# Four tiles of stationary operands placed at the other end of SBUF in a decoder layer

## The chip, the core and the metric

The program runs on one core of a Trainium2 chip. A core has TensorE for matmuls, VectorE, ScalarE and GpSimd for work on vectors, SyncE for issuing DMAs, a memory of 128 partitions by 224 KiB (SBUF) for operands and a small one (PSUM) into which matmuls accumulate. The metric is the device time of one execution in microseconds.

## What is computed

The reference is one decoder layer on 256 tokens of width 2048, in float32:

```python
x = x + 0.5 * swiglu(rms_norm(x, ffn1_norm), ffn1_w_gate, ffn1_w_up, ffn1_w_down)    # D_FF = 5632
h = rms_norm(x, mix_norm)
proj = h @ w_in                     # split among three groups of heads
...                                 # gated linear attention, sparse attention, attention to 256 memory tokens
x = x + concat([o_gla, o_nsa, o_mem]) @ w_out
x = x + 0.5 * swiglu(rms_norm(x, ffn2_norm), ffn2_w_gate, ffn2_w_up, ffn2_w_down)
return rms_norm(x, final_norm)
```

The matmul work is in the two feed-forward networks (three matrices of 2048 by 5632 each), the projections `w_in`, `w_mem_kv` and `w_out`.

## The kernel before

Each float32 operand of a large product is split into two fp32r parts, a rounded value and the rest (`h` and `l` for weights), and a product becomes three matmuls: `mm3` (L301 to L304) multiplies the high part of the stationary side by the high part of the moving side (L302), by the low part (L303), and the low part of the stationary side by the high part of the moving side (L304). I call such three matmuls a triple. The weights stream: a DMA brings a chunk of 128 by 1024 into a tile `r`, ScalarE rounds it into `h` (L288), VectorE takes the difference `l` (L289), and both are moving operands, 512 columns at a time. The stationary side is 128 by 128: activations.

Those activations stay in SBUF in tiles of 16 KB per partition, 16 blocks of 128 by 256, made by the helper `t16` from the pool `p_t16`, which has four buffers and is open for the whole program. The pairs follow one another: `hh`, `hl` (input of the first network), `sh`, `sl` (sums and differences of its quarters), `xh`, `xl` (input of the projections), `oh`, `ol` (output of the heads), `zh`, `zl` and again `sh`, `sl` (second network); `sa`, `sb` and `gfin` borrow a buffer too. Blocks of 128 columns of them are what the weight load reads. Of the ten projections of `xh`, `xl` eight have 512 columns, one 296 and one 256.

The network runs in 11 slabs of 512 hidden columns. A slab after the first multiplies with seven products in place of eight for three quarters of its depth, and between its groups it puts in the down products of the slab before. For those the hidden values lie in the tile `gx`, 8 KB from a stage pool, high half and low half side by side, and `gx` is the stationary side. The seven products and the plain ones use `hh`, `hl`, `sh`, `sl` (`zh`, `zl` in the second network). A product of six matmuls is `product7`, the down products are `fill`.

The pools are opened in this order: `const`, `keep` (with `acc`, the residual), `p_t16`, `sm` (small values), and then, one stage after another, the pools of the first network, of the mixing part and of the second network. The stage pools are closed and opened again by `stage`, which means that a tile of a new stage waits for the last users of the earlier tile on the same bytes. All pools without a side grow from the low end of SBUF. In the compiled program the first 16 KB are taken by descriptors; `ident` of `const` begins at 0x4080, `acc` at 0x7ca0, the four buffers of `p_t16` at 0xbe00, 0xfe00, 0x13e00 and 0x17e00, `sm` at 0x1be00 and the stage pools at 0x1c340: in the networks `r` from there, `h` from 0x27340, `l` from 0x2d340, `gx` at 0x33340 and `wk` (tiles such as `c` and `g`) from 0x35340 to 0x37b40. In the mixing part `mT` and `qT` lie at multiples of 64 bytes and the two `kT` at 0x368a0 and 0x370e0, that is 32 past a multiple of 64; the last tile ends at 0x37d20. The range that the allocator may use ends at 0x37fe0, 32 bytes below 224 KiB.

The pools' line and the helper that takes tiles from the pool are:

```python
    const, keep, p_t16 = mk("const"), mk("keep"), mk("t16", 4)
...
    def t16(name, dt=F32R):
        return p_t16.tile([128, 16, 256], dt, name=name, tag="t16")
```

Of the kernel before, what the change touches and what calls it, by code (L numbers as in the profile page):

```python
# [186 lines left out]
def _body(tc, A):  # L187
# [1 line left out]
    act, dve, pool, pe = nc.scalar, nc.vector, nc.gpsimd, nc.tensor  # L189
    ctx = ExitStack()  # L190
    mk = lambda n, b=1, **k: ctx.enter_context(tc.tile_pool(name=n, bufs=b, **k))
    const, keep, p_t16 = mk("const"), mk("keep"), mk("t16", 4)
    sm = mk("sm", 3)
    P, sizes = {}, {}

# [1028 lines left out]
```

## Time and profile before

| | |
|---|---|
| median of 3 runs | 1881.18 us (1879.79 to 1882.1) |
| profiled execution | 1881.27 us |
| its span, first to last instruction | 1879.5 us |
| TensorE busy, matmul | 1840.5 us, 98% of the span |
| TensorE busy, weight load | 1486.1 us, 79% |
| VectorE busy | 1642.3 us, 87% |
| ScalarE busy | 1086.0 us, 58% |
| DMA | 397.34 MB, 211 GB/s |
| mean granted clock of TensorE | 0.994 of full |

The profile is one execution. Busy time of TensorE is the sum of matmuls whose ends are modelled and which overlap, so a matmul of 389 ns may follow another after 229; the distance from start to start is what counts, and I call it the spacing. The weight load has an engine row of its own (PEld), since it runs beside the matmul before.

### The profile page before, as it was taken

Reading aid. Unit: us, or ns where it says so; the run is one execution under the profiler, and the core shown is the slowest. Engines: PE = TensorE matmul, PEld = TensorE weight load, DVE = VectorE, ACT = ScalarE, POOL = GpSimd, SP = SyncE. Lnnn points to the kernel's source line nnn. Section 1 sums busy time; section 2 is a strip of 40 time slices with the busy share of each in tenths; the row PEclk is TensorE's granted clock in tenths of the full one; section 3 lists DMA queues with packets and bytes.
Section 4 is the critical chain, followed back from the end, with each engine's and each line's share of the span. In section 5 each row is a group of like instructions: output and inputs, shape, how many; then the busy total and the mean of one; then the engine's idle time right before and its main releaser. Section 6 shows DMA issues by size and latency. Waiting matters only on the chain.

```text
span 1879.5 us, 23784 instructions
## 1 busy us (share of the span) xinstructions
PE 1840.5 (98%) x8465; PEld 1486.1 (79%) x8465; DVE 1642.3 (87%) x2101; ACT 1086.0 (58%) x1376; POOL 84.6 (5%) x109
## 2 busy tenths in 40 slices
PE   8989999999999999999999999999999999999997
PEld 5868888888888877777777787888888888888885
DVE  7999999999999985576577854999999999999995
ACT  7446665656565656533456744566556655666563
POOL 0000000000000000001010000000000000000000
PEclk9999999999999999999999999999999999999999
DMA  9768777767776754545744453876777677767771
GB/s 333 228 190 261 253 225 235 247 202 226 236 249 197 229 169 158 188 150 177 247 157 130 163 181 117 295 239 209 213 237 255 203 214 238 253 201 216 239 246 49
DMA packets 111655, 397.34 MB, mean 211 GB/s; under 512 B 12592, under 2 KB 12848, under 8 KB 111408
## 3 DMA queue, kind: packets, MB, share of 16 engines
q1 hardware_dynamic: 102896, 364.36, 55.4%
q0 software_dynamic: 8640, 31.46, 9.7%
q8 instruction: 66, 1.08, 0.2%
q14 instruction: 53, 0.43, 0.1%
HBM read 393.68 MB, written 2.10 MB: 211 GB/s over the span
## 4 chain that ended last, share of the span: by engine, by line
PE 91%; DVE 5%; ACT 1%; issue 1%; POOL 1%; ACTq 0%; POOLq 0%; DVEq 0%
PE pm L303 20%; PE pm L302 20%; PE pm L304 20%; PE px L303 8%; PE px L302 8%; PE px L304 8%; DVE l L289 1%; PE pt L391 1%; PE pm L854 1%; PE px L819 0%; POOL y L326 0%; PE pt L339 0%; DVE exg L910 0%; PE po L1047 0%; POOL y L325 0%
## 5 line engine op out<-in xcount | busy, mean ns | idle before, releaser
L288 ACT ACTIVATE h<-r 128x1024 fp32r<-128x1024 f32 (+1 forms) x838 | 877.8, 1052 | 660.3 <-PE pm L304 491.6
L289 DVE TENSOR_TENSOR l<-r,h 128x1024 fp32r<-128x1024 f32 (+1 forms) x838 | 990.7, 1207 | 137.7 <-ACT h L288 129.3
L303 PE MATMUL px<-l,gx 128*128 128x512 f32 x624 | 243.2, 390 | 1.7 <-DVE l L289 1.7
L302 PE MATMUL px<-h,gx 128*128 128x512 f32 x624 | 243.2, 390 | 0.0
L304 PE MATMUL px<-h,gx 128*128 128x512 f32 x624 | 242.9, 389 | 0.0
L303 PE MATMUL pm<-l,sh 128*128 128x512 f32 x480 | 191.9, 400 | 2.3 <-DVE l L289 2.3
L302 PE MATMUL pm<-h,sh 128*128 128x512 f32 x480 | 190.1, 397 | 0.3 <-ACT h L288 0.3
L304 PE MATMUL pm<-h,sl 128*128 128x512 f32 x480 | 188.0, 392 | 0.0
L303 PE MATMUL pm<-l,hh 128*128 128x512 f32 x364 | 144.8, 398 | 3.6 <-DVE l L289 3.6
L302 PE MATMUL pm<-h,hh 128*128 128x512 f32 x364 | 142.4, 395 | 4.4 <-ACT h L288 4.4
L303 PE MATMUL pm<-l,zh 128*128 128x512 f32 x364 | 144.3, 396 | 0.1
L302 PE MATMUL pm<-h,zh 128*128 128x512 f32 x364 | 143.3, 394 | 0.0
L304 PE MATMUL pm<-h,zl 128*128 128x512 f32 x364 | 142.2, 391 | 0.0
L304 PE MATMUL pm<-h,hl 128*128 128x512 f32 x364 | 142.2, 391 | 0.0
L303 PEld LDWEIGHTS px<-l,gx 128*128 128x128 f32 x624 | 117.2, 188 | 26.7 <-DVE l L289 2.4
L302 PEld LDWEIGHTS px<-h,gx 128*128 128x128 f32 x624 | 117.2, 188 | 25.4 <-ACT h L288 0.2
L304 PEld LDWEIGHTS px<-h,gx 128*128 128x128 f32 x624 | 117.2, 188 | 24.2
L303 PE MATMUL pm<-l,xh 128*128 128x512 f32 (+2 forms) x320 | 120.7, 377 | 1.5 <-DVE l L289 1.5
L302 PE MATMUL pm<-h,xh 128*128 128x512 f32 (+2 forms) x320 | 121.3, 380 | 0.0
L304 PE MATMUL pm<-h,xl 128*128 128x512 f32 (+2 forms) x320 | 121.0, 379 | 0.0
L402 DVE SCALAR_TENSOR_TENSOR acc<-px,acc 128x512 f32<-128x512 f32 x156 | 106.9, 685 | 8.3 <-PE px L304 7.9
L302 PEld LDWEIGHTS pm<-h,sh 128*128 128x128 f32 x480 | 90.6, 189 | 20.5 <-ACT h L288 0.9
(329 smaller groups left out, 2641.0 us busy)
## 6 DMA issues: line engine op xcount, KB each, us to landing
r<-ffn1u SPq DMA_DIRECT2D x88, 512.0 KB, 4.9
r<-ffn1d SPq DMA_DIRECT2D x88, 512.0 KB, 4.9
r<-ffn2u SPq DMA_DIRECT2D x88, 512.0 KB, 4.7
r<-ffn2d SPq DMA_DIRECT2D x88, 512.0 KB, 4.8
r<-ffn1g SPq DMA_DIRECT2D x87, 512.0 KB, 5.0
r<-ffn2g SPq DMA_DIRECT2D x87, 512.0 KB, 5.1
r<-wout SPq DMA_DIRECT2D x32, 512.0 KB, 3.4
r<-ffn1u POOLq DMA_DIRECT2D x30, 512.0 KB, 7.3
```

The source lines that it names most:

```text
L288: act.activation(h[:, sl], r[:, sl], AF.Copy)
L289: dve.tensor_sub(l[:, sl], r[:, sl], f(h[:, sl]))
L302: pe.matmul(out, ah, wh, start=first, stop=False)
L303: pe.matmul(out, ah, wl, start=False, stop=False)
L304: pe.matmul(out, al, wh, start=False, stop=last)
L391: pe.transpose(pt[:, k], g[:, k * 128:k * 128 + 128], ident)
L402: dve.scalar_tensor_tensor(a, pd, 0.5, a, op0=ALU.mult, op1=ALU.add)
L854: pe.matmul(pcs[n][32 * p:32 * p + 32], flats[n][:, c * 4 + p], r[:, p * 256:p * 256 + 256], start=c == 0, stop=c == 7, tile_position=(0, ...
```

## The change

The pool of the four tiles is opened with a side. Its tiles then come from the high end of SBUF, above everything that the other pools take; the pools that are opened after it (`sm` and the stage pools) move down by the 64 KB that it leaves. `const` and `keep` stay in place. Nothing else is edited.

```diff
-    const, keep, p_t16 = mk("const"), mk("keep"), mk("t16", 4)
+    const, keep, p_t16 = mk("const"), mk("keep"), mk("t16", 4, side="right")
```

## Rows read from the trace of the kernel before

**Rows 1.** Table of stages: stretch, its us, busy us by engine, granted clock, DMA.
```profile
130.00:200.00 70.00, 65.16 (x278) 52.82 (x277) 68.01 (x83) 37.59 (x39) 2.59 (x3) 0.95 0.72 230
200.00:300.00 100.00, 100.00 (x448) 82.47 (x447) 98.49 (x100) 65.06 (x71) 4.31 (x5) 1.00 0.75 247
700.00:760.00 60.00, 56.59 (x287) 45.34 (x288) 36.00 (x59) 37.78 (x71) 3.64 (x6) 0.97 0.46 155
1100.00:1180.00 80.00, 78.34 (x347) 62.24 (x347) 43.33 (x54) 38.94 (x60) 0.89 (x2) 0.98 0.45 160
```

**Rows 2.** Chain that ended last, by engine, share of the span.
```profile
PE 91%; DVE 5%; ACT 1%; issue 1%; POOL 1%; ACTq 0%; POOLq 0%; DVEq 0%
```

**Rows 3.** Groups by line, one matmul of each triple: count | busy us, mean ns.
```profile
L303 PE MATMUL pm<-l,sh 128*128 128x512 f32 x480 | 191.9, 400 | 2.3 <-DVE l L289 2.3
L303 PE MATMUL pm<-l,hh 128*128 128x512 f32 x364 | 144.8, 398 | 3.6 <-DVE l L289 3.6
L303 PE MATMUL pm<-l,zh 128*128 128x512 f32 x364 | 144.3, 396 | 0.1
L303 PE MATMUL pm<-l,xh 128*128 128x512 f32 (+2 forms) x320 | 120.7, 377 | 1.5 <-DVE l L289 1.5
L303 PE MATMUL pm<-l,oh 128*128 128x512 f32 x128 | 51.2, 400 | 0.0
L303 PE MATMUL px<-l,hh 128*128 128x512 f32 x40 | 15.8, 394 | 0.0
L303 PE MATMUL px<-l,zh 128*128 128x512 f32 x40 | 15.8, 394 | 0.0
L303 PE MATMUL px<-l,gx 128*128 128x512 f32 x624 | 243.2, 390 | 1.7 <-DVE l L289 1.7
L303 PE MATMUL pm<-l,gx 128*128 128x512 f32 x80 | 32.0, 400 | 0.0
```

**Rows 4.** Timeline of TensorE, first and last matmul of three runs: start, duration.
```profile
250.27 0.39 PE L302 MATMUL pm<-h,hh 128*128 128x512 f32 x1
...
265.15 0.39 PE L304 MATMUL pm<-h,sl 128*128 128x512 f32 x1
...
304.60 0.39 PE L302 MATMUL px<-h,gx 128*128 128x512 f32 x1
...
307.10 0.39 PE L304 MATMUL px<-h,gx 128*128 128x512 f32 x1
...
1838.53 0.39 PE L302 MATMUL pm<-h,gx 128*128 128x512 f32 x1
...
1843.75 0.39 PE L304 MATMUL pm<-h,gx 128*128 128x512 f32 x1
```

**Rows 5.** Table of stages for the first and last of these runs.
```profile
250.26:265.16 14.90, 14.90 (x67) 12.22 (x66) 14.54 (x17) 8.52 (x9) 0.00 (x0) 1.00 0.45 135
1838.52:1843.75 5.23, 5.23 (x25) 4.32 (x24) 4.04 (x6) 1.95 (x2) 0.00 (x0) 1.00 0.00 0
```

**Rows 6.** Instructions of single lines: duration ns min/median/max, first and last start.
```profile
L303 PEld LDWEIGHTS px<-l,gx x624: 187/188/190, 71.5 to 1821.4; 128*128 128x128 f32 x156
L303 PEld LDWEIGHTS pm<-l,sh x480: 187/188/337, 63.6 to 1825.5; 128*128 128x128 f32 x160
L339 PEld LDWEIGHTS pt<-ident,acc x64: 137/140/143, 710.2 to 1172.5; 128*128 128x128 f32 x64
L391 PEld LDWEIGHTS pt<-ident,c x160: 137/141/231, 134.4 to 1847.8; 128*128 128x128 f32 x160
L999 PE MATMUL px<-kT,qT x16: 379/380/484, 978.5 to 1043.7; 128*128 128x256 f32 x16
L1126 PE MATMUL px<-mT x16: 378/380/459, 1062.8 to 1075.2; 128*128 128x256 f32 x16
```

## What I predict

> **What bounds the kernel now.** I read three views, in this order. First the table of stages: in a stretch of a feed-forward network TensorE is busy all the time at the full granted clock, while VectorE, the next one, is at 98.49 of 100 us and ScalarE at 65 [rows 1]. Then the chain that ended last: 91% of it is TensorE [rows 2], so the end is set by the number of matmuls times the spacing of their starts, and a wait only counts where TensorE stands still. Then the matmuls themselves: the groups of one line of the helper [rows 3] are one matmul of each triple, so the tiles that the change moves (hh, hl, sh, sl, xh, xl, zh, zl, oh, ol) are the stationary side of 480 + 364 + 364 + 320 + 128 + 40 + 40 = 1736 triples, that is 5208 matmuls; gx, which the change moves with the stage buffers, serves 624 + 80 = 704 triples, 2112 matmuls.
>
> **What the change removes, adds and moves.** It names no operation, no loop and no DMA, so the instruction counts stay. The four tiles are one pool that is open for the whole program; no other pool has ever used its bytes, before or after, so no buffer is handed over that was not handed over before. `sm` and the stage pools slide down together by 65,536 bytes and keep their places relative to each other, so each stage tile still lands on the same earlier tiles. I cost the waits of the buffers at nothing for that reason. Of the queues, SP keeps its DMAs and POOL its accumulating ones; a DMA to another address of the same 128 partitions has the same packets. What is left are the addresses, and an address can only matter in how long an operand takes to read or write.
>
> The largest reader is the matmul with its weight load, and here the trace has two values for the same shape. A run of 66 matmuls on hh, hl, sh and sl starts at 250.27 and its last one at 265.15 us: 14.88 us / 65 = 228.9 ns from start to start [rows 4, 5]. A run of 24 on gx goes from 1838.53 to 1843.75: 5.22 / 23 = 227.0 ns, and 12 on gx in the middle of a network from 304.60 to 307.10: 2.50 / 11 = 227.3 ns [rows 4, 5]. So gx is about 2 ns quicker per matmul, at the same moving buffers, clock and width. The weight load isn't what differs: 188 ns median for gx and for sh [rows 6], some 40 ns below the spacing, which hides it.
>
> What could make those 2 ns? The place is one candidate (gx lies at the top, 0x33340, the four tiles lie below the stages, from 0xbe00). Against it speaks that the four tiles span 64 KB themselves, and that the matmuls on hh and those on zh, which lie 32 KB apart, take 394 ns alike where they accumulate in px [rows 3]. The contents are another (gx holds the hidden values), and so is the layout (gx keeps both halves in one tile, the others in two). The change touches the first only. I take 0 ns as the value, and keep both ends: -2 ns if the new place has the spacing of gx, +2 ns if the move costs as much as the two places differ now.
>
> The second thing an address can alter is its offset. The four tiles start at a multiple of 512 bytes now. The allocator's usable range ends 32 bytes below 224 KiB, so from the other end they start at 0x27fe0 or a little lower; a block of 128 weights then starts 32 bytes past a multiple of 64. The trace has such operands today: acc lies at 0x7ca0, 32 past a multiple of 64, and the weight load of its transposes takes 140 ns median, that of the tile c, at a multiple of 64, 141 [rows 6]. With the moving side it is the same: kT lies 32 bytes off and mT doesn't, and the 256-wide matmuls take 380 ns and 380 [rows 6]. So I cost the offset at nothing too; if this cover were gone, the load has 40 ns of slack before the spacing grows. ScalarE's and VectorE's writes into the four tiles are few beside their work on h and l, and both engines have slack [rows 1].
>
> One rule of the Trainium skill bears on the 2 ns. The rows show equal loads and unequal spacings [rows 4, 6]. The page TensorE: Matmul & The Clock Gate (Part 2: What happens when you issue a matmul) says that TensorE has two independent read ports, so that loading the next weights takes nothing from the running matmul. By that rule the place of the stationary side is worth nothing and the time stays; by the row, read as an effect of the place, it would fall as in the first rival. The rule doesn't explain why gx is quicker.
>
> **The sum.** Profiled time 1881.27 us, span 1879.5, so 1.8 us lie around it. Changes: operations 0, waits 0, spacing 5208 x 0 + 2112 x 0, offset 0. That gives 1881.27; the median of the runs shown is 1881.18 (1879.79 to 1882.1), and I forecast **1881.2 us**. What can still move without a cause: the granted clock is 0.95 of full over 130 to 200 us, 0.97 over 700 to 760 and 0.98 over 1100 to 1180 [rows 1], that is 3.5, 1.8 and 1.6 us of lost full speed where TensorE had stood still for parts of the stretch; it falls to 1.2 from 2.4 GHz there. One such fall more or less is worth about 2 us, so the forecast alone reaches from 1878.5 to 1884.
>
> **The rivals.** *Faster: the quick spacing belongs to the place.* The four tiles then cover 0x27fe0 to 0x37fe0, where gx lies today, and gx goes down to 0x23340. From the groups, 8 of the 10 projections are 512 wide, so 5016 of the 5208 matmuls are; 5016 x -2 ns = -10.0 us, and gx loses 2112 x 2 ns = +4.2. Net -5.8: **1875.4 us**. If only the upper half of the four tiles gains, it is -5.0 + 4.2, and that lies within the forecast. For it: the rows show the 2 ns. Against it: the buffers of hh and zh lie 32 KB apart and take the same 394 ns [rows 3], and contents and layout explain it as well. VectorE wouldn't stop it, since it has 1.5 us of 100 left and TensorE would need less than 1% of it.
>
> *Slower: the 32-byte offset costs on every load.* Place: the weight loads of the four tiles in all three products. If the block of 512 bytes takes one piece more and TensorE's start waits for that, the price is at most what the trace shows between two sources, 2 ns: 5016 x 2 = +10.0 us, **1891.2 us**. It decides from 3.8 us / 5016 = 0.75 ns per matmul. For it: only that the fp32r loads of this shape are nowhere 32 bytes off in the trace. Against it: acc and kT, which are, and the 40 ns of slack.
>
> *The change isn't only one of addresses.* If the planner that orders the instructions sees other buffer edges, a wait could come or go. The forecast takes it that it does not, because no bytes change hands; this would show as another number of waits and either sign. I count its small chance with the two others.
>
> **How the numbers follow.** The forecast has 0.72, the faster rival with the favourable mishaps 0.15, the slower one with the others 0.13. About 0.2%, 3.8 us, is what a measurement of this kernel can tell from no change, and the forecast lies inside it while both rivals lie outside. So faster 0.15, same 0.72, slower 0.13. The range takes the forecast and the faster rival whole and the smaller half of the slower one's price: 1874 to 1886.5. Some 0.1 of the slower rival is left out above, and a few hundredths below.
>
> **What would show it.** Right: the same instruction counts, a slab run of 66 matmuls still at 228.9 ns, 24 on gx still at 227.0, weight loads at 188. The faster rival shows as runs on hh and sh below 228.2 and gx near 229; the slower one as runs above 229.7, perhaps with loads above 188. A different order shows as other waits of TensorE at the groups of h and l. I am wrong if the spacing of the matmuls moves by 0.75 ns or more on average, or if a new stall of a few us appears where TensorE already stands at the edges of the stages.

## The result

The change makes the kernel slower: 1908.84 us (1908.16 to 1910.8) against 1881.64 (1879.79 to 1884.06), a ratio of 1.0145 with a 95% interval of 1.0132 to 1.0157. I had forecast 1881.2 us, and the time lies above the whole range. The profiled execution took 1908.7 us; its span grew from 1879.5 to 1906.9, by 27.4 us.

The page of after, span and busy time by engine, then the chain that ended last by engine:

```profile
span 1906.9 us, 23784 instructions
PE 1869.0 (98%) x8465; PEld 1486.0 (78%) x8465; DVE 1647.2 (86%) x2101; ACT 1086.4 (57%) x1376; POOL 84.8 (4%) x109
...
PE 90%; DVE 5%; ACT 1%; issue 1%; POOL 1%; DMA 0%; ACTq 0%; POOLq 0%; SPq 0%; DVEq 0%
```

The number of instructions is that of before on every engine, and TensorE's order is that of before. Weight loads are as busy as they were (1486.0 against 1486.1 us), and so are the other engines to within 5 us. Only the matmuls grew, by 28.5 us, and the chain is still TensorE's [rows 2].

The groups that answer to [rows 3]: count | busy us, mean ns | idle time before them and what ended it.

```profile
L303 PE MATMUL px<-l,gx 128*128 128x512 f32 x624 | 245.8, 394 | 1.6 <-DVE l L289 1.6
L303 PE MATMUL pm<-l,sh 128*128 128x512 f32 x480 | 193.8, 404 | 2.3 <-DVE l L289 2.3
L303 PE MATMUL pm<-l,hh 128*128 128x512 f32 x364 | 146.2, 402 | 3.5 <-DVE l L289 3.4
L303 PE MATMUL pm<-l,zh 128*128 128x512 f32 x364 | 145.9, 401 | 0.1
```

Every group is 4 or 5 ns longer per matmul, gx too, and the idle time ahead of them is what it was, to 0.2 us. So no wait explains the loss: each matmul starts a little later after the one ahead of it. The timeline of TensorE shows the spacing (start, duration): a run of 66 on the four tiles, a run of 12 on gx, and the run of 24 on gx with its ninth matmul.

```profile
252.80 0.39 PE L302 MATMUL pm<-h,hh 128*128 128x512 f32 x1
...
267.97 0.40 PE L304 MATMUL pm<-h,sl 128*128 128x512 f32 x1
...
308.09 0.40 PE L302 MATMUL px<-h,gx 128*128 128x512 f32 x1
...
310.62 0.40 PE L304 MATMUL px<-h,gx 128*128 128x512 f32 x1
...
1864.46 0.40 PE L302 MATMUL pm<-h,gx 128*128 128x512 f32 x1
...
1866.31 0.39 PE L304 MATMUL pm<-h,gx 128*128 128x512 f32 x1
...
1869.71 0.39 PE L304 MATMUL pm<-h,gx 128*128 128x512 f32 x1
```

The 66 take 15.17 us / 65 = 233.4 ns each, where before had 228.9 [rows 4]. The 12 on gx take 2.53 / 11 = 230.0, where it was 227. The run of 24 is the telling one: its first eight spacings are 1.85 / 8 = 231.3, the last fifteen 3.40 / 15 = 226.7. So gx itself is as quick as it was; it starts slow behind the four tiles and recovers after eight matmuls. The fills of twelve do the same: by the starts, the mean over 150 of them is 231.4 ns for the first eight spacings and 226.7 for the last three, so most of a fill is spent in the slow part.

The table of stages for these runs (stretch, us, busy us by engine, granted clock, DMA share, GB/s), and the weight loads (min/median/max ns):

```profile
252.79:267.98 15.19, 15.19 (x67) 12.21 (x66) 14.54 (x17) 8.53 (x9) 0.00 (x0) 1.00 0.43 129
1864.45:1869.72 5.27, 5.27 (x25) 4.32 (x24) 3.99 (x6) 1.95 (x2) 0.00 (x0) 1.00 0.00 0
...
L303 PEld LDWEIGHTS px<-l,gx x624: 186/188/189, 72.0 to 1847.0; 128*128 128x128 f32 x156
L303 PEld LDWEIGHTS pm<-l,sh x480: 186/188/337, 64.0 to 1851.2; 128*128 128x128 f32 x160
```

The clock is 1.00, the run of 66 has the VectorE and ScalarE work that it had [rows 5], and a load takes 188 ns as before [rows 6].

The sum closes. Over the whole trace the mean spacing (starts less than 300 ns apart, from the starts themselves) rose from 229.14 to 233.33 ns for hh, hl, sh, sl, zh and zl, 3774 of them (+15.8 us), from 227.02 to 230.48 for gx, 2075 (+7.2), and from 229.9 to 233.4 for the other 512-wide matmuls, 1200 (+4.1). That is +27.1 of the 27.4 us.

### The profile page after: what moved, and what is told of

It reads as the page before. It is cut to its first block, busy times and chain, and to the rows that moved or that the text cites. A ratio compares the mean times of both kernels' runs of the same rounds, so it can differ in the third digit from the quotient of the medians.

```text
span 1906.9 us, 23784 instructions
## 1 busy us (share of the span) xinstructions
PE 1869.0 (98%) x8465; PEld 1486.0 (78%) x8465; DVE 1647.2 (86%) x2101; ACT 1086.4 (57%) x1376; POOL 84.8 (4%) x109
## 4 chain that ended last, share of the span: by engine, by line
PE 90%; DVE 5%; ACT 1%; issue 1%; POOL 1%; DMA 0%; ACTq 0%; POOLq 0%; SPq 0%; DVEq 0%
PE pm L303 20%; PE pm L302 20%; PE pm L304 20%; PE px L303 8%; PE px L302 8%; PE px L304 8%; DVE l L289 1%; PE pt L391 1%; PE px L819 0%; PE pm L854 0%; POOL y L326 0%; DMA r<-win_q 0%; DVE acc L402 0%; DVE exg L910 0%; PE pt L339 0%
## 5 line engine op out<-in xcount | busy, mean ns | idle before, releaser
L303 PEld LDWEIGHTS pm<-l,sh 128*128 128x128 f32 x480 | 90.8, 189 | 22.4 <-DVE l L289 2.9
```

The source lines that it names most:

```text
L303: pe.matmul(out, ah, wl, start=False, stop=False)
```

## The experiments

All of them move tiles and do nothing else: the padding is a tile that nobody writes. Addresses are given modulo 512 where they matter. Before has the four tiles at 0 and the moving tiles h, l and gx at 0x140; after has the four tiles at 0x1e0 and the others at 0x140. The **distance** is the start of a stationary tile minus the start of h. The times of before in the four sets were 1882.47, 1881.36, 1881.07 and 1881.57 us.

**First set: the offset, the place or the distance?** Three theories: the four tiles are slow because they start 32 bytes past a multiple of 64 (my slower rival); because they lie at the other end (place); or because their distance from the moving tiles changed, from 0xc0 to 0xa0.

The change, but the four tiles at a multiple of 64:

```diff
-    const, keep, p_t16 = mk("const"), mk("keep"), mk("t16", 4)
-    sm = mk("sm", 3)
+    const, keep, gap = mk("const"), mk("keep"), mk("gap", side="right").tile([128, 8], F32, name="gap")
+    p_t16, sm = mk("t16", 4, side="right"), mk("sm", 3)
```

> As after, but 32 unused bytes at the very end move the four tiles from 0x27fe0 to 0x27fc0, a multiple of 64; nothing else moves. Offset theory (what costs is that the blocks of weights start 32 past a multiple of 64): about 1882 us, triples on hh and sh back at 687 ns. Place theory (what costs is the high end of the memory): 1908 us, triples at 700 ns. Theory of the distance (what counts is the start of the weights against the start of the moving tiles, modulo 512): the difference goes from 0xa0 to 0x80, neither value of before (0xc0) nor of after; a time of its own between 1870 and 1910 us.

Measured 1903.22 us, ratio 1.0111 [1.0096, 1.0126]. The offset theory falls: with the offset gone most of the loss stayed.

The place of before, with the offset and the distance 0xa0 of after:

```diff
-    const, keep, p_t16 = mk("const"), mk("keep"), mk("t16", 4)
-    sm = mk("sm", 3)
+    const, keep, gap = mk("const"), mk("keep"), mk("gap").tile([128, 8], F32, name="gap")
+    p_t16, gap2, sm = mk("t16", 4), mk("gap2").tile([128, 8], F32, name="gap2"), mk("sm", 3)
```

> As before, but 32 unused bytes ahead of the four tiles and 32 behind them: they start at 0xbe20, 32 past a multiple of 64, at the low end, and the stage tiles move up by 64, to another multiple of 64. Offset theory: 1908 us. Place theory: 1881 us. Theory of the distance: it is 0xa0 modulo 512, that of after, so 1908 us as well.

Measured 1909.20 us, 1.0144 [1.0129, 1.0159]: the whole loss, without the move. The place theory falls.

Before, with the stages moved up until the distance is 0:

```diff
-    sm = mk("sm", 3)
+    gap, sm = mk("gap").tile([128, 48], F32, name="gap"), mk("sm", 3)
```

> As before, but 192 unused bytes between the four tiles and the stage tiles: both start at multiples of 512 now, so their distance is 0 modulo 512, as that of gx is in the kernel before. Offset theory and place theory: 1881 us, 687 ns a triple. Theory of the distance: the triples on hh and sh take what those on gx take, 681 ns, and the time falls by 1672 x 6 ns = 10 us, to 1871 us.

Measured 1874.37 us, 0.9963 [0.9950, 0.9976]: faster than before.

The change, with the distance brought to 0, both kinds of tile 32 bytes past a multiple of 64:

```diff
-    const, keep, p_t16 = mk("const"), mk("keep"), mk("t16", 4)
-    sm = mk("sm", 3)
+    const, keep, p_t16 = mk("const"), mk("keep"), mk("t16", 4, side="right")
+    gap, sm = mk("gap").tile([128, 40], F32, name="gap"), mk("sm", 3)
```

> As after, with the four tiles 32 past a multiple of 64, but the stage tiles moved up by 160 bytes, so that they start 32 past a multiple of 64 too and the distance is 0 modulo 512. Offset theory: 1908 us or more, since the moving tiles have the offset now as well. Place theory: 1908 us. Theory of the distance: 1871 to 1881 us.

Measured 1874.74 us, 0.9964 [0.9950, 0.9978]. Place and offset are those of after, and the time is 34 us below it. The distance decides. The run of 66 in the timeline of the layout with distance 0:

```profile
252.85 0.39 PE L302 MATMUL pm<-h,hh 128*128 128x512 f32 x1
...
267.59 0.39 PE L304 MATMUL pm<-h,sl 128*128 128x512 f32 x1
```

14.74 / 65 = 226.8 ns: the four tiles are now as quick as gx. And gx always had the distance 0, before and after.

**Second set and two more: the curve.** The edit is that of the third experiment with another number of columns of padding: 112 (distance 0x100), 64 (0x1c0), 32 (0x40) and 16 (0x80); later 40 (0x20), 56 (0x1e0, that is 0xe0 modulo 256) and 24 (0x60); and 56 together with the change's side="right" (0xc0).

> The layout of before with 448 bytes of padding behind the four tiles: their start stays a multiple of 512, the stage buffers start 0x100 past one, so the distance (start of the stationary tile minus start of the moving one) is 0x100 modulo 512. Known so far: distance 0 gave 1874.4 and 1874.7, 0xc0 1881, 0x80 1903, 0xa0 1909 us. Theory M512 (only the distance modulo 512 counts, and it is a collision of the two reads that grows away from 0): another time than at 0, between 1880 and 1915. Theory M256 (the pattern repeats every 256 bytes): 1874.5, as at distance 0. Additive theory (each of the two starts has its own cost): the four tiles have the start of before, so only the stage's part can change; no number.

> The layout of before with 256 bytes of padding behind the four tiles: distance 0x1c0 modulo 512. M256: 0x1c0 is 0xc0 again, so 1881 to 1882, with triples as before (226, 229, 232 ns). M512: a time of its own; near distance 0 from the other side, 1874 to 1882 if the effect is the same on both sides.

> The layout of before with 128 bytes of padding: distance 0x40 modulo 512. Between distance 0 (1874.5) and 0x80 (1903): a smooth effect gives about 1889; a repeat every 256 bytes that is the same on both sides gives 0xc0 mirrored, 1881.

> The layout of before with 64 bytes of padding: distance 0x80, with the four tiles at a multiple of 512 below the stages, where the run at 0x27fc0 above them with the same distance took 1903.2. Distance theory: 1903 (1900 to 1906). Additive theory: the part of the stage start 0x180 was in the run with the four tiles at 0xbe20, 1909; with their start at a multiple of 512 as in before no number follows, but 1903 would be an accident. Place theory: near 1881.

> The layout of before with 160 bytes of padding: distance 0x20. Distance theory: a time of its own between 1874 and 1909; by its neighbours 0 (1874.4) and 0x40 (1903) about 1889. Any theory in which only multiples of 64 matter: that of 0x00 or of 0x40.

> The layout of before with 224 bytes of padding: distance 0xe0 modulo 256, between 0xc0 (1881.4) and 0 (1874.5). If the effect counts 32 bytes (as 0x20 at 1901 says, against 1874.5 at 0) and 0 is the one quick place: between 1876 and 1905. If -0x20 is as quick as 0: 1874 to 1878.

> The layout of before with 96 bytes of padding: distance 0x60, between 0x40 and 0x80, both 1903. All distances that are not near 0 slow the matmuls: 1900 to 1910. If there is a second quick place half way round: under 1885.

> The change as it is (four tiles at the other end, at 0x27fe0), with 224 bytes of padding ahead of the stages, so that the distance is 0xc0 modulo 256 as in before. Distance theory: the change without its side effect, 1881.5 (1880 to 1883), runs on hh and sh at 226, 229, 232 ns. If the move has any cost of its own, what is above 1881.5 is that cost.

| distance modulo 256 | layouts (0x... as run) | time, us | mean spacing on the four tiles, ns |
|---|---|---|---|
| 0x00 | 0 below, 0 above, 0x100 | 1874.37, 1874.74, 1874.78 | 227.3 |
| 0x20 | 0x20 | 1900.97 | 233.1 |
| 0x40 | 0x40 | 1903.01 | 233.2 |
| 0x60 | 0x60 | 1906.83 | 234.0 |
| 0x80 | 0x80 above, 0x80 below | 1903.22, 1903.28 | 232.7 |
| 0xa0 | after, and its distance below | 1908.84, 1909.20 | 233.3 |
| 0xc0 | before, 0x1c0, the change with 0xc0 | 1881.64, 1881.41, 1881.96 | 229.1 |
| 0xe0 | 0x1e0 | 1900.62 | 232.9 |

Above and below mean where the four tiles lie. Layouts with the same distance modulo 256 agree to 0.6 us whatever their place and their starts, also where the distances are 256 apart, so the pattern repeats every 256 bytes; the theory that it takes 512 falls, and so does one in which each start has a cost of its own, which would need three accidents. The times don't follow the last column strictly, since gx, whose own distance is 0 in all of these, is slowed behind the four tiles by different amounts: its mean by the starts is 228.0 ns at 0x60 and 230.5 in after. Two places are quick, 0 and, less so, 0xc0; by 32 bytes either way from 0 it is already 26 us slower, so my reading between neighbours for 0x20 (1889) was wrong. The change at before's distance is 1.0000 of before [0.9990, 1.0009]: the move itself costs nothing, within 1.9 us. Its groups are those of [rows 3] to 2 ns:

```profile
L303 PE MATMUL px<-l,gx 128*128 128x512 f32 x624 | 243.2, 390 | 1.8 <-DVE l L289 1.8
L303 PE MATMUL pm<-l,sh 128*128 128x512 f32 x480 | 191.8, 400 | 2.3 <-DVE l L289 2.3
L303 PE MATMUL pm<-l,hh 128*128 128x512 f32 x364 | 144.7, 398 | 3.1 <-DVE l L289 3.0
L303 PE MATMUL pm<-l,zh 128*128 128x512 f32 x364 | 143.5, 394 | 0.3 <-DVE l L289 0.2
```

**Third set: which pair?** All of these start from the layout with distance 0 (48 columns of padding) and put one kind of tile 0x80 off. In the networks' pools:

```diff
-FFN_SB = {"raw": (11, 1024), "hi": (6, 1024), "lo": (6, 1024), "gx": (1, 2048), "wk": (5, 512)}
+FFN_SB = {"raw": (11, 1024), "hi": (6, 1024), "lo": (6, 1024), "pad": (1, 32), "gx": (1, 2048), "wk": (5, 512)}
...
-            sizes[n] = size
+            sizes[n] = P[n].tile([128, size], F32, name=name + n) and size if "pad" in n else size
```

That is gx alone. For l alone, a pad stands ahead of "lo" and a second one behind it; for h alone, ahead of "hi" and behind it.

> The layout with distance 0 (1874.4 us) and, in the two networks, 128 bytes of padding ahead of gx, so that gx alone has the distance 0x80 to the moving tiles h and l; the four tiles keep 0. Distance theory: the 2112 matmuls on gx now take the repeating pattern of the runs at 0x80 (241, 233, 231, 232, 228, 230 ns, mean 232.5) in place of 226.7 ns: 2112 x 5.8 = +12.3, so 1886.7 us, or half of it where runs of 12 are too short for the pattern to set in; runs on hh and sh stay at 227. Rival (only the four tiles matter, gx is quick for its layout): 1874.4, gx at 227.

Measured 1889.63 us, 1.0048 [1.0031, 1.0064]: 15.3 us more than distance 0, where 12.3 was expected. The run of 24 on gx, first and last matmul, and its stage row:

```profile
1847.07 0.40 PE L302 MATMUL pm<-h,gx 128*128 128x512 f32 x1
...
1852.43 0.39 PE L304 MATMUL pm<-h,gx 128*128 128x512 f32 x1
...
1847.06:1852.44 5.38, 5.38 (x25) 4.35 (x24) 4.06 (x6) 1.99 (x2) 0.00 (x0) 1.00 0.00 0
```

5.36 / 23 = 233.0 ns, and no byte was moved by a DMA meanwhile (last two columns). So gx isn't quick for its layout, and DMA traffic isn't needed for the loss. Runs of 12 on the four tiles between two runs on gx, still at distance 0, rose to 229.6 (from the starts), as gx had in after, while their runs of 66 stayed at 227.2: that carrying over is the part that I hadn't counted.

> The layout with distance 0 and, in the two networks, 128 bytes of padding ahead of and behind the buffers of l, so that l alone is 0x80 off the four tiles and gx. Of a triple one matmul streams l. Theory that the load of the next weights collides with the stream that is running: the load of hl runs beside the stream of l, so the spacing from the second to the third matmul of a triple grows, the two others stay near 227; 1992 such matmuls in the networks at about +5.8 ns are +11.6, 1886 us; between a third and all of the +28 of distance 0x80 if the disturbance carries over to the next matmuls. Rival (the collision is with the writes of ScalarE and VectorE into h and l, not with the stream): no pattern by place in the triple.

Measured 1904.31 us, 1.0123 [1.0108, 1.0139], more than the upper end that I gave.

> The layout with distance 0 and, in the two networks, 128 bytes of padding ahead of and behind the buffers of h, so that h alone is 0x80 off. Collision of the next load with the running stream: the first and third matmul of a triple stream h, so the first and third spacings grow and the second stays near 227, where l alone grew the second. If any one pair that is off disturbs all three (carry-over without end): all three near 232 as at 0x80, 1903.

Measured 1885.30 us, 1.0018 [1.0008, 1.0027]. And the four tiles of 128 bytes more each, which puts one of each pair off:

```diff
-        return p_t16.tile([128, 16, 256], dt, name=name, tag="t16")
+        return p_t16.tile([128, 4128], dt, name=name, tag="t16")[:, :4096].rearrange("p (a b) -> p a b", a=16)
```

> The layout with distance 0 and buffers of the four tiles that are 128 bytes longer each, so that of each pair one tile starts at a multiple of 256 and the other 0x80 past it: the low tiles (hl, xl, zl, and sl of the first network) are off, and in ol's pair and in the second network's sh, sl the high ones are. Collision of the next load with the running stream: where the low tile is off, its load runs beside the second matmul of the triple, so the second spacing grows; where the high tile is off, its loads run beside the third and the first, so those two grow. Collision of a load with its own matmul's stream: the third spacing grows where the low tile is off, the first and the second where the high one is. Time: 5016 matmuls of which a third (low off) or two thirds (high off, about a fourth of the triples) at +5.8 ns: 5016 x 0.42 x 5.8 = +12, 1886 us, more if it carries over.

Measured 1894.81 us, 1.0073 [1.0058, 1.0088], where 1886 was expected. The instructions of single lines on zh and zl, first, second and third of a triple (min/median/max ns); the modelled duration is some 160 to 164 ns above the distance to the next start, and at distance 0 its median is 390 for all three. First h alone, then the low stationary tile alone, then l alone:

```profile
L302 PE MATMUL pm<-h,zh x364: 392/393/506, 1175.4 to 1840.2; 128*128 128x512 f32 x182
L303 PE MATMUL pm<-l,zh x364: 387/388/502, 1176.0 to 1840.5; 128*128 128x512 f32 x182
L304 PE MATMUL pm<-h,zl x364: 388/391/398, 1176.3 to 1840.7; 128*128 128x512 f32 x182
```

```profile
L302 PE MATMUL pm<-h,zh x364: 386/389/793, 1178.9 to 1849.2; 128*128 128x512 f32 x182
L303 PE MATMUL pm<-l,zh x364: 390/396/792, 1179.4 to 1849.4; 128*128 128x512 f32 x182
L304 PE MATMUL pm<-h,zl x364: 390/397/628, 1179.8 to 1849.6; 128*128 128x512 f32 x182
```

```profile
L302 PE MATMUL pm<-h,zh x364: 392/397/761, 1181.5 to 1858.7; 128*128 128x512 f32 x182
L303 PE MATMUL pm<-l,zh x364: 389/395/795, 1182.1 to 1858.9; 128*128 128x512 f32 x182
L304 PE MATMUL pm<-h,zl x364: 392/393/628, 1182.4 to 1859.1; 128*128 128x512 f32 x182
```

With h off, the first and, by little, the third spacing grow (232.5 and 228.5 ns by the starts) and the second doesn't (226), as a collision of the next weight load with the running stream has it. With the low stationary tile off, the first stays at 227, the second grows to 232.5 as that theory says, and the third to 234 as its rival says (a load against the stream of its own matmul). With l off, the trace has at least three patterns that each last for long stretches: 227, 234, 226 (from 170 to 270 us), the clean form of the theory; 236, 234, 230 (from 1400 to 1800 us), where all three are disturbed; and 231, 230, 233 on average (from 345 to 395 us). So the pair that is off does show by its position, but a disturbed matmul also disturbs the next ones, and the two theories can't be told apart by that. Which load collides with which stream stays open, and what happens inside the memory was not seen.

One rival can be settled from the traces: that the collision is with the other engines' accesses (ScalarE and VectorE write h and l all the time) or with DMA. In the output projection, with oh and ol stationary, there is a stretch in which VectorE, ScalarE and GpSimd have no instruction and no DMA moves a byte. The stage rows from the start of its first matmul to that of the last, for before, after and the layout with distance 0 (columns as in [rows 1]):

```profile
1158.74:1165.15 6.41, 6.41 (x30) 5.26 (x28) 0.00 (x0) 0.00 (x0) 0.00 (x0) 1.00 0.00 0
1172.94:1179.24 6.30, 6.30 (x29) 5.07 (x27) 0.00 (x0) 0.00 (x0) 0.00 (x0) 1.00 0.00 0
1158.14:1164.49 6.35, 6.35 (x30) 5.26 (x29) 0.00 (x0) 0.00 (x0) 0.00 (x0) 1.00 0.00 0
```

They hold 28, 27 and 28 spacings: 228.9, 233.3 and 226.8 ns, the values of the whole runs, and the stretch is longer than the eight matmuls that a disturbance lasted on gx. So the loss needs no other engine and no DMA. What is left, by exclusion, are TensorE's own reads: of the stationary tile by the weight load and of the moving tile by the stream.

## Why the prediction was wrong

**What bounds the kernel** was right: TensorE, and the spacing times the count. It is why 3 to 4 ns per matmul became 27 us with no engine waiting longer.

**Operations, order, waits, loads: 0.** Right, each of them: same instructions, same idle time, loads at 188.

**The place at 0 ns.** Right: 1.0000 [0.9990, 1.0009] at equal distance. The faster rival, which gave the place the 2 ns of gx, falls; gx's 2 ns are real but belong to its distance of 0, which none of my three candidates (place, contents, layout) was.

**The offset at 0 ns.** Taken alone this holds too: four tiles at 32 past a multiple of 64 gave 1874.74. The step that failed is the one ahead of both, "an address can only matter in how long an operand takes to read or write". That looks at each tile by itself. The term that was missing is the pair: the change moved the four tiles and the stages by amounts that differ by 32 bytes modulo 256, from distance 0xc0 to 0xa0, and that is the whole 27 us: the spacing on the four tiles rose from 229.1 to 233.3 ns, and with before's distance restored the time was 1881.96 us. I had both starts in the text and never subtracted them.

**The cover.** The rows on acc and kT [rows 6] compared durations of loads and of short matmuls, one tile at a time. The load takes 188 ns at every distance, so it is the wrong gauge, and the 40 ns of slack hid nothing: the loss shows in the start of the next matmul, not in the load.

**The slower rival** had the sign and named what would show it, runs of 66 above 229.7 ns, but not the mechanism (the offset fell in the first run) nor the size. Its price was capped at the 2 ns between two sources of the trace. That was no cap, since before's distance happens to be the second best of the eight; the four tiles lost 4.2 ns. It also left gx at 227, while gx lost 3.5 ns behind the four tiles, another 7 us.

**The rule of the Trainium skill**, that loading the next weights takes nothing from the running matmul (TensorE: Matmul & The Clock Gate, Part 2: What happens when you issue a matmul), gave an unchanged time. Here the spacing of the same matmuls went from 227.3 to 234.0 ns by moving tiles alone, also where nothing but TensorE worked, so the measurement speaks against the rule for these operands. The Trainium skill's page SBUF — State Buffer (Who interferes with whom) says that TensorE never waits on anyone. The stretch without other engines agrees as far as those are meant, since the loss is there in full (233.3 ns) without them.

**What is left to gain** is small: at distance 0 the four tiles have 227.3 ns. The three layouts with it are 0.35% faster than before, each interval below 1. My expectation of 1871 took the 2 ns of an undisturbed run for all 5016 matmuls; by the starts it was 1.8 for six of the tiles and 1.2 for the other 512-wide matmuls. VectorE is close behind; the row of the layout with distance 0 that answers to [rows 1] has it at 98.65 of 100 us:

```profile
200.00:300.00 100.00, 100.00 (x450) 82.72 (x449) 98.65 (x101) 65.64 (x72) 4.31 (x5) 1.00 0.73 242
```

## What to carry to other kernels

Where a kernel is bound by a chain of matmuls, treat the address of a tile as a relation: before a pool is moved, padded or resized, subtract the start of the moving tile from that of the stationary one, modulo 256, and keep the difference where it was, or try 0. Shown is this for 512-wide fp32r matmuls with a weight load each, at multiples of 32 bytes; other widths and types were not compared. A change that "only" moves memory is tested with one padded twin that restores the old difference; if that twin has the old time, the move itself was free. And when two groups of equal shape differ by a steady 2 ns, look for what differs between the pairs of operands before setting it aside.

## What the hardware showed that I had not expected

- The start-to-start time of 512-wide fp32r matmuls at full clock depends on the distance between stationary and moving tile modulo 256: 227.3 ns at 0, 229.1 at 0xc0, 232.7 to 234.0 at the six others. The loads don't show it: they stay at 188 ns. It is there with every other engine and DMA silent (228.9, 233.3 and 226.8 ns at 0xc0, 0xa0 and 0).
- It has a memory: a pair at distance 0 runs at 231.3 for its first eight matmuls behind a pair at 0xa0, then at 226.7. With l alone off, different patterns (227, 234, 226 and 236, 234, 230, for two) each hold for long stretches of the same run.
- One third of a triple that is off can cost as much as all of it: l alone, in the networks only, takes 1904.31 us against 1903.28 for the four tiles at 0x80 throughout, where gx keeps its distance of 0, while h alone, two thirds of a triple, takes 1885.30.
